# A squared-ReLU MLP in Strassen–Winograd products: one more running sum copied out of PSUM by ScalarE, the blocks of x made later, six weight tiles tagged singly

## The chip, the cores and the metric

The kernel runs on one core of a Trainium2 chip. The metric is the device time of one execution in microseconds (us). Three runs of the kernel before gave 1105.33, 1103.91 and 1101.88 us, a median of 1103.91. The core has a matrix engine (TensorE, PE in the rows), a vector engine (VectorE, DVE), a scalar engine (ScalarE, ACT), GpSimd (POOL) and SyncE (SP). The first four run instruction streams of their own and wait for each other on semaphores; in this kernel SP does nothing but issue transfers, and POOL also issues transfers that add what they bring to a tile. Matrix products land in PSUM, which the kernel uses as eight banks; everything else stands in SBUF.

## The reference

The model has two layers, d_model 1024, 512 positions, one sequence, float32. Layer 0 mixes by stick-breaking attention, layer 1 by a gated linear recurrence (RG-LRU). Each is followed by the MLP that this change is about:

```
x = x + y                                    # y: the mixer's output
h = rms_norm(x, norm_mlp[layer])             # x * rsqrt(mean(x*x) + 1e-6) * g
u = relu(h @ w1)                             # 512x1024 @ 1024x4096
x = x + (u * u) @ w2                         # 512x4096 @ 4096x1024
...
return rms_norm(x, norm_final)               # after the second layer
```

## The kernel before, in words

**Precision.** A float32 matrix is split into a high part (a cast to the type fp32r) and a low part (the matrix less its high part). A product is then three matmuls: high by high, high by low, low by high. So every operand costs a cast on ScalarE and a subtraction on VectorE; for weights these are `wh` (L971) and `wl` (L972) in `operand`, for the hidden activations `split` (L822: L825 on ScalarE, L826 on VectorE).

**The MLP (class `Mlp`, L729).** The 4096 hidden features are worked through in four quarters (`NQ`). A quarter has a first product (x by w1, then relu and square) and a second product (the squares by w2, added to the result tiles `c`).

- The first quarter's first product is dense: `squared(c)` (L790), eight chunks of 128 features, 24 matmuls of 512 columns each. Between the chunks the loop in `quarters` also puts the sums of squares for the norm (`self.sq.chunk`) and, from chunk 4 on, the *blocks of x*: `sums_of_x` (L853) scales x by the norm's gain on ScalarE and forms four block sums on VectorE, `halves_of_sums` (L876) splits these into high and low parts, and `replace` (L891), after the first second product, puts one of them where `xgh` was.
- The first products of quarters 1 to 3 are done by `up` (L896) as seven Strassen–Winograd products P1 P5 P6 P3 P7 P2 P4 of 24 matmuls each, in two halves p = 0 and 1. P1, P6, P7 and P4 add up in one PSUM bank, the running sum X; P5 and P3 in another, V; P2 stands alone, W. An intermediate value of a running sum is needed by its own: after P1, P5 and P6 ScalarE copies the bank to a tile `kept` (L922). After P3 and P7 VectorE subtracts bank and kept tile (L931, L933), after P2 it adds them (L933), and ScalarE takes relu (L934) and square (L788). P4 adds to X after P7, so it can't begin before VectorE has read X for P7.
- Each half then ends in a finishing chain: a split of three of the blocks (128 x 1536), four sums of blocks (`sums`, L828, on VectorE at L835) and two more splits of 128 x 1024. The hidden tile `u` has one buffer, which the two halves share.
- The second product is `down` (L1026): fourteen products (seven for each half g of the hidden quarter) of 12 matmuls of 512 columns. The orders stand in `ORDERS`. P5 of half 1 needs the last splits. With g = 1 the PSUM sums are scaled and added to `c` (`collect`, L1009: VectorE L1015, ScalarE L1018).

**Weights.** A product's weight is a block of w1 or w2 or a running sum of blocks. `load` (L943) issues three blocks of 512 KB on SP for each half; b21 comes through `raw` tiles in `block`. A sum of blocks is made in place by VectorE (L991), or, for P7 and P4 (the *far* products), by a transfer from POOL that accumulates (L986). The tiles have tags b11, b12 and b22 with two buffers each.

**Order.** The order of matmuls is the program's. On the other engines a list scheduler (the Tile framework) places each instruction by its own estimate of when operands are ready and by priority, which follows program order unless a `high_priority` block raises it; `issue_after` holds an instruction behind another one. Engines then run their queues strictly in order, so the instruction at the head of a queue holds up all behind it.

The last quarter of each layer goes through the `prepare` path of `down`, which prepares each weight three products ahead, and ends with `end`: in layer 0 the transposition into x for the next mixer, in layer 1 the final norm.

Of the kernel before, what the change touches and what calls it, by code (L numbers as in the profile page):

```python
# [48 lines left out]
def hybrid_encoder(  # L49
# [679 lines left out]
    class Mlp:  # L729
# [28 lines left out]
        def __init__(self, ctx, layer):  # L758
# [9 lines left out]
            self.u, self.lows, self.s3 = {}, {}, []  # L768
# [18 lines left out]
        def square(self, t):  # L787
            A.activation(t, t, AF.Square)  # L788
# [33 lines left out]
        def split(self, p, i, of, to):  # L822
            h, l = (t[:, i, to, :] for t in self.places(p))
            u = self.u[p][:, i, of, :]
            A.copy(h, u)  # L825
# [27 lines left out]
        def sums_of_x(self, k):  # L853
# [3 lines left out]
            for c in (k, C // 2 + k):  # L857
                g = col(f"mlp{self.layer}")[:, c : c + 1]
                A.activation(x[c], x[c], AF.Identity, scale=g)
            V.tensor_tensor(v[:, hi], u[:, hi], v[:, hi], ALU.subtract)  # L860
# [35 lines left out]
        def up(self, q4, p, unit, far):  # L896
# [3 lines left out]
            for name in ("P1", "P5", "P6", "P3", "P7", "P2", "P4"):  # L900
# [19 lines left out]
                if name in ("P1", "P5", "P6"):  # L920
                    t = work.tile([P, S], F32, tag="sq" if name == "P1" else "r", name="kept")
                    A.copy(t, ps)  # L922
                    kept[name] = t.rearrange("p (i n) -> p i n", i=2)
                    continue
                slot, one, op = {
                    "P3": (1, "P6", ALU.subtract), "P7": (2, "P5", ALU.subtract),
                    "P2": (0, "P1", ALU.add), "P4": (3, None, None),
                }[name]
                t = u[:, :, slot, :]
                if name == "P3":  # L930
                    V.tensor_tensor(t, three, kept[one], op)  # L931
                elif one:
                    V.tensor_tensor(t, kept[one], three, op)  # L933
                A.activation(t, t if one else three, AF.Relu)  # L934
                self.square(t)
                if name == "P2":
                    self.split(p, slice(0, 2), slice(0, 3), slice(0, 3))
            self.sums(p, slice(0, 2))
            for i in range(2):
                self.split(p, i, slice(0, 4), slice(3, 7))  # L940


        def load(self, src, far=()):  # L943

            unit = {"src": src}
            for tag in ("b11", "b12", "b22"):
                t = self.bp.tile([P, 2, S], F32, tag=tag, name=tag)
                nc.sync.dma_start(out=t.rearrange("p j n -> p (j n)"), in_=src(tag))
                unit[tag] = t
            return unit  # L950

        def from_up(self, q4, p):
            return self.load(
# [72 lines left out]
        def down(self, q4, units, far, end=None):  # L1026
# [19 lines left out]
            if end is None:  # L1046
                for at in order:
                    product(*at)
# [453 lines left out]
```

## Time and profile before

The profiled execution took 1100.71 us, of which its span, first to last instruction, is 1099.0 us; the median of the runs, 1103.91 us, is 3.2 us above it.

| view | value |
|---|---|
| TensorE busy | 1053.4 us, 96% of the span, mean granted clock 0.983 |
| VectorE busy | 867.1 us, 79% |
| ScalarE busy | 676.4 us, 62% |
| GpSimd busy | 205.1 us, 19% |
| layer 0, `down` of the first quarter and after (293 to 337 us) | TensorE 41.14 of 44.00 us, VectorE 34.98, ScalarE 21.97, clock 0.96 |
| layer 0, `up` of quarter 1 (337 to 381 us) | TensorE 41.30 of 44.00, VectorE 34.55, ScalarE 32.30, clock 1.00 |
| layer 0, `down` of quarter 1 (381 to 420 us) | TensorE 37.84 of 39.00, VectorE 32.49, ScalarE 15.50, clock 1.00 |
| layer 1, `down` of the first quarter (790 to 839 us) | TensorE 42.41 of 49.00, VectorE 37.36, ScalarE 18.55, clock 0.90 |
| layer 1, `up` of quarter 1 (839 to 882 us) | TensorE 40.32 of 43.00, VectorE 34.47, ScalarE 30.12, clock 0.97 |

A row of a timeline reads: start in us, length in us, engine, source line, operation, output tile and input tiles, shape, how many instructions in a row (x2), and in brackets the idle time of that engine before it and what ended that idle time. A row of the chain (the chain of work that ended last) gives start, length and what worked. L1004 are the matmuls of `down`, L913 those of `up`.

### The profile page before, as it was taken

Reading aid. Unit: us, or ns where it says so; the run is one execution under the profiler, and the core shown is the slowest. Engines: PE = TensorE matmul, PEld = TensorE weight load, DVE = VectorE, ACT = ScalarE, POOL = GpSimd, SP = SyncE. Lnnn points to the kernel's source line nnn. Section 1 sums busy time; section 2 is a strip of 40 time slices with the busy share of each in tenths; the row PEclk is TensorE's granted clock in tenths of the full one; section 3 lists DMA queues with packets and bytes.
Section 4 is the critical chain, followed back from the end, with each engine's and each line's share of the span. In section 5 each row is a group of like instructions: output and inputs, shape, how many; then the busy total and the mean of one; then the engine's idle time right before and its main releaser. Section 6 shows DMA issues by size and latency. Waiting matters only on the chain.

```text
span 1099.0 us, 15815 instructions
## 1 busy us (share of the span) xinstructions
PE 1053.4 (96%) x5868; PEld 912.1 (83%) x5868; DVE 867.1 (79%) x1120; ACT 676.4 (62%) x1025; POOL 205.1 (19%) x240
## 2 busy tenths in 40 slices
PE   9999999999989999999999999999979999999987
PEld 7888888888879879889877777888858888988975
DVE  7888787749876987987898778964966886887887
ACT  6767676748645745745745487855834754753655
POOL 2444443400000000000002563000000000000004
PEclk9999999999999999999999999999989999989999
DMA  7745454427366565565742784252255665655604
GB/s 237 196 119 161 116 141 114 159 87 279 89 161 152 129 181 144 134 180 146 209 77 77 176 207 134 63 187 77 58 123 164 147 140 157 156 126 153 178 3 113
DMA packets 53405, 155.22 MB, mean 141 GB/s; under 512 B 8784, under 2 KB 9552, under 8 KB 53328
## 3 DMA queue, kind: packets, MB, share of 16 engines
q1 hardware_dynamic: 43536, 120.13, 34.2%
q0 software_dynamic: 9216, 33.56, 18.7%
q8 instruction: 46, 0.75, 0.3%
q10 hardware_dynamic: 576, 0.52, 0.2%
q14 instruction: 31, 0.25, 0.1%
HBM read 132.17 MB, written 4.19 MB: 124 GB/s over the span
## 4 chain that ended last, share of the span: by engine, by line
PE 73%; DVE 13%; ACT 6%; issue 4%; DMA 2%; POOL 1%; SPq 0%; ACTq 0%; DVEq 0%; POOLq 0%
PE ps_t L913 7%; PE ps_z L913 7%; PE ps_acc L1004 6%; PE ps_t L1004 6%; PE ps_o L1004 5%; PE ps_z L1004 4%; PE ps_acc L212 4%; PE ps_acc L210 4%; PE ps_acc L211 4%; PE ps_o L913 3%; DVE wl L972 2%; ACT wh L971 2%; PE ps_o L210 2%; DVE b L991 2%; PE ps_o L212 2%
## 5 line engine op out<-in xcount | busy, mean ns | idle before, releaser
L971 ACT CAST wh<-b 128x1024 fp32r<-128x1024 f32 x168 | 174.3, 1049 | 186.6 <-DVE b L991 74.3
L972 DVE TENSOR_TENSOR wl<-b,wh 128x1024 fp32r<-128x1024 f32 x168 | 204.3, 1223 | 75.6 <-ACT wh L971 74.4
L986 POOL DMA_DIRECT2D b<-in_w_dn x30 | 26.3, 878 | 383.9 <-DVE wl L972 109.6
L198 ACT CAST wh<-raw 128x512 fp32r<-128x512 f32 (+2 forms) x88 | 69.5, 819 | 37.2 <-DMA raw<-in_w_in 10.4
L210 PE MATMUL ps_acc<-xgh,wh 128*128 128x512 f32 x208 | 85.0, 409 | 0.2 <-ACT wh L179 0.2
L205 DVE TENSOR_TENSOR wl<-raw,wh 128x512 fp32r<-128x512 f32 (+2 forms) x78 | 71.1, 938 | 16.5 <-ACT wh L198 16.3
L211 PE MATMUL ps_acc<-xgh,wl 128*128 128x512 f32 x208 | 81.5, 392 | 0.3 <-DVE wl L180 0.3
L212 PE MATMUL ps_acc<-xgl,wh 128*128 128x512 f32 x208 | 81.6, 392 | 0.1
L562 DVE TENSOR_TENSOR_SCAN scan<-keep,later 128x128 f32<-128x128 f32 (+1 forms) x64 | 58.5, 915 | 18.2 <-ACT keep L552 9.6
L986 POOL DMA_DIRECT2D b<-in_w_up x24 | 20.9, 871 | 277.3 <-DVE b L991 210.1
L991 DVE TENSOR_TENSOR b<-b,b 128x1024 f32<-128x1024 f32 x58 | 70.3, 1220 | 0.3
L566 POOL TENSOR_TENSOR w<-w,scan 128x128 f32<-128x128 f32 (+1 forms) x64 | 52.1, 815 | 55.4 <-DVE scan L562 52.5
L913 PE MATMUL ps_t<-xgh,wh 128*128 128x256 f32 x144 | 43.1, 299 | 10.8 <-ACT u L934 10.8
L972 DVE TENSOR_TENSOR wl<-raw,wh 128x1024 fp32r<-128x1024 f32 x28 | 34.2, 1223 | 18.9 <-ACT wh L971 18.8
L913 PE MATMUL ps_z<-xgh,wh 128*128 128x256 f32 x144 | 42.5, 295 | 5.4 <-DVE u L933 2.7
L835 DVE TENSOR_TENSOR u<-u 128x512 f32<-128x512 f32 (+1 forms) x80 | 46.5, 582 | 1.3
L212 PEld LDWEIGHTS ps_acc<-xgl,wh 128*128 128x128 f32 x208 | 39.0, 188 | 8.9 <-DVE xgl L119 0.5
L913 PE MATMUL ps_t<-low,wh 128*128 128x256 f32 x160 | 44.8, 280 | 0.0
L210 PEld LDWEIGHTS ps_acc<-xgh,wh 128*128 128x128 f32 x208 | 39.2, 189 | 6.6 <-ACT wh L179 0.5
L211 PEld LDWEIGHTS ps_acc<-xgh,wl 128*128 128x128 f32 x208 | 39.3, 189 | 6.3 <-DVE wl L180 0.9
L826 DVE TENSOR_TENSOR sl<-u,sh 128x1024 fp32r<-128x1024 f32 (+2 forms) x26 | 33.4, 1304 | 12.1 <-ACT sh L825 12.1
L551 ACT ACTIVATE w<-ps_z,rp 128x128 f32<-128x128 f32 (+3 forms) x56 | 29.7, 531 | 21.1 <-PE ps_z L544 18.4
(426 smaller groups left out, 3560.8 us busy)
## 6 DMA issues: line engine op xcount, KB each, us to landing
b<-in_w_dn SPq DMA_DIRECT2D x48, 512.0 KB, 5.7
b<-in_w_up SPq DMA_DIRECT2D x36, 512.0 KB, 4.0
b<-in_w_dn POOLq DMA_DIRECT2D x30, 512.0 KB, 5.5
b<-in_w_up POOLq DMA_DIRECT2D x24, 512.0 KB, 5.5
raw<-in_w_m SPq DMA_DIRECT2D x16, 512.0 KB, 3.6
raw<-in_w_dn SPq DMA_DIRECT2D x16, 512.0 KB, 4.3
raw<-in_w_in SPq DMA_DIRECT2D x16, 512.0 KB, 5.1
raw<-in_w_qk SPq DMA_DIRECT2D x12, 512.0 KB, 3.8
```

What stands on the lines that cost most here:

```text
L198: A.copy(wh[:, k, :], raw[:, k, :])
L205: V.tensor_tensor(wl[:, k, :], raw[:, k, :], f(wh[:, k, :]), ALU.subtract)
L210: PE.matmul(ps, wh, ah, start=start, stop=False)
L211: PE.matmul(ps, wl, ah, start=False, stop=False)
L212: PE.matmul(ps, wh, al, start=False, stop=stop)
L562: V.tensor_tensor_scan(sc[:, S - n : S][:, ::-1], keep[:, :n][:, ::-1], later[:, S - n :][:, ::-1], 1.0, ALU.mult, ALU.max,)
L566: G.tensor_tensor(wt, wt, sc[:, S - n + 1 : S + 1], ALU.mult)
L913: PE.matmul(ps[:, i * HS : (i + 1) * HS], m, y, start=new and i == k == n == 0, stop=i == 1 and k == C // 2 - 1 and n == 2, skip_group_che ...
L971: A.copy(wh, raw)
L972: self.cut = V.tensor_tensor(wl, raw, f(wh), ALU.subtract)
L991: self.sum = V.tensor_tensor(raw, raw, unit[to], ALU.add)
L1004: PE.matmul(ps, m, y[:, jj, cols], start=first and n == 0, stop=last and n == 2, skip_group_check=not new,)
```

## The change

1. In `up`, P7's running sum X is copied out by ScalarE like those of P1, P5 and P6 (into a `kept` tile of tag "sq"); VectorE then subtracts two SBUF tiles instead of a tile and a bank.
2. In `up`, the relu and square of P4 stand in a `high_priority` block, and so do the four sums and the last two splits.
3. `sums_of_x` and `halves_of_sums` move from the loop over `squared` into the `down` of the first quarter (after its steps 2 to 5), and `replace` goes after its step 7. `issue_after` puts the scalings behind the last high split and the first subtraction behind the last low split. `sq.chunk` is held behind the square before it.
4. The weight tiles b11, b12, b22 of the two halves have six tags b0 to b5 with one buffer each; `FROM_DOWN` and `FROM_UP` say which tile follows which. Loads are issued singly: four of the next quarter's at step 10 of `down` and two after it; of `down`'s six, three after the first half of `up` and three after the second.
5. The turn of the PSUM banks begins anew in every quarter; layer 0's last `down` uses the order "mid" instead of "last"; `prepare` holds a block sum behind the last weight difference but one (`cuts[-2]`); in layer 1's last quarter P7's block sums, too, are made by POOL's accumulating transfer.

```diff
@@ -765,7 +765,7 @@
             self.turns = count()
             self.blocks = ExitStack()
             self.bp = self.blocks.enter_context(tc.tile_pool(name=f"blocks{layer}", bufs=2))
-            self.u, self.lows, self.s3 = {}, {}, []
+            self.u, self.lows, self.s3, self.slots = {}, {}, [], None
 
             self.s41 = self.bp.tile([P, C // 2, S], F32R, tag="s41", name="s41", bufs=1)
 
@@ -785,7 +785,7 @@
             return self.u[p]
 
         def square(self, t):
-            A.activation(t, t, AF.Square)
+            self.squares = A.activation(t, t, AF.Square)
 
         def squared(self, c):
 
@@ -822,7 +822,7 @@
         def split(self, p, i, of, to):
             h, l = (t[:, i, to, :] for t in self.places(p))
             u = self.u[p][:, i, of, :]
-            A.copy(h, u)
+            self.high = A.copy(h, u)
             self.ready = V.tensor_tensor(l, u, f(h), ALU.subtract)
 
         def sums(self, p, i):
@@ -856,8 +856,10 @@
             u, v = x[k], x[C // 2 + k]
             for c in (k, C // 2 + k):
                 g = col(f"mlp{self.layer}")[:, c : c + 1]
-                A.activation(x[c], x[c], AF.Identity, scale=g)
-            V.tensor_tensor(v[:, hi], u[:, hi], v[:, hi], ALU.subtract)
+                with tc.issue_after(self.high.ins):
+                    A.activation(x[c], x[c], AF.Identity, scale=g)
+            with tc.issue_after(self.ready.ins):
+                V.tensor_tensor(v[:, hi], u[:, hi], v[:, hi], ALU.subtract)
             V.tensor_tensor(u[:, hi], u[:, lo], u[:, hi], ALU.subtract)
             V.tensor_tensor(u[:, lo], v[:, hi], u[:, lo], ALU.subtract)
             V.tensor_tensor(v[:, lo], u[:, lo], v[:, lo], ALU.add)
@@ -917,50 +919,79 @@
                                 skip_group_check=not new,
                             )
                 three = ps.rearrange("p (i n) -> p i n", i=2)
-                if name in ("P1", "P5", "P6"):
-                    t = work.tile([P, S], F32, tag="sq" if name == "P1" else "r", name="kept")
+                if name in ("P1", "P5", "P6", "P7"):
+
+                    tag = "sq" if name in ("P1", "P7") else "r"
+                    t = work.tile([P, S], F32, tag=tag, name="kept")
                     A.copy(t, ps)
                     kept[name] = t.rearrange("p (i n) -> p i n", i=2)
+                if name in ("P1", "P5", "P6"):
                     continue
-                slot, one, op = {
-                    "P3": (1, "P6", ALU.subtract), "P7": (2, "P5", ALU.subtract),
-                    "P2": (0, "P1", ALU.add), "P4": (3, None, None),
+                slot, x, y, op = {
+                    "P3": (1, three, kept.get("P6"), ALU.subtract),
+                    "P7": (2, kept.get("P5"), kept.get("P7"), ALU.subtract),
+                    "P2": (0, kept.get("P1"), three, ALU.add),
+                    "P4": (3, three, None, None),
                 }[name]
                 t = u[:, :, slot, :]
-                if name == "P3":
-                    V.tensor_tensor(t, three, kept[one], op)
-                elif one:
-                    V.tensor_tensor(t, kept[one], three, op)
-                A.activation(t, t if one else three, AF.Relu)
-                self.square(t)
-                if name == "P2":
-                    self.split(p, slice(0, 2), slice(0, 3), slice(0, 3))
-            self.sums(p, slice(0, 2))
-            for i in range(2):
-                self.split(p, i, slice(0, 4), slice(3, 7))
-
-
-        def load(self, src, far=()):
-
-            unit = {"src": src}
-            for tag in ("b11", "b12", "b22"):
-                t = self.bp.tile([P, 2, S], F32, tag=tag, name=tag)
-                nc.sync.dma_start(out=t.rearrange("p j n -> p (j n)"), in_=src(tag))
-                unit[tag] = t
-            return unit
-
-        def from_up(self, q4, p):
-            return self.load(
-                lambda tag: w_up[self.layer, q4 - 1, p, *self.SOURCES[tag]].rearrange(
-                    "p k n -> p (k n)"
-                )
+                with tc.high_priority() if name == "P4" else nullcontext():
+                    if op:
+                        V.tensor_tensor(t, x, y, op)
+                    A.activation(t, t if op else three, AF.Relu)
+                    self.square(t)
+                    if name == "P2":
+                        self.split(p, slice(0, 2), slice(0, 3), slice(0, 3))
+            with tc.high_priority():
+                self.sums(p, slice(0, 2))
+                for i in range(2):
+                    self.split(p, i, slice(0, 4), slice(3, 7))
+
+
+
+
+        FROM_DOWN = {
+            (0, "b11"): (0, "b22"), (0, "b12"): (1, "b22"), (0, "b22"): (0, "b12"),
+            (1, "b11"): (1, "b12"), (1, "b12"): (0, "b11"), (1, "b22"): (1, "b11"),
+        }
+        FROM_UP = {
+            (0, "b11"): (0, "b11"), (0, "b12"): (0, "b12"), (1, "b11"): (0, "b22"),
+            (1, "b12"): (1, "b22"), (0, "b22"): (1, "b12"), (1, "b22"): (1, "b11"),
+        }
+
+        def units(self, sources, come_from):
+
+            if self.slots is None:
+                self.slots = {at: i for i, at in enumerate(come_from)}
+            else:
+                self.slots = {at: self.slots[old] for at, old in come_from.items()}
+            return [{"src": src} for src in sources]
+
+        def load(self, units, *ats):
+            for g, tag in ats:
+                t = self.bp.tile([P, 2, S], F32, tag=f"b{self.slots[g, tag]}", name=tag, bufs=1)
+                nc.sync.dma_start(out=t.rearrange("p j n -> p (j n)"), in_=units[g]["src"](tag))
+                units[g][tag] = t
+
+        def from_up(self, q4):
+            return self.units(
+                [
+                    lambda tag, p=p: w_up[self.layer, q4 - 1, p, *self.SOURCES[tag]].rearrange(
+                        "p k n -> p (k n)"
+                    )
+                    for p in range(2)
+                ],
+                self.FROM_DOWN,
             )
 
-        def from_down(self, q4, g):
-            return self.load(
-                lambda tag: w_dn[self.layer, q4, g, *self.SOURCES[tag]].rearrange(
-                    "p j n -> p (j n)"
-                )
+        def from_down(self, q4):
+            return self.units(
+                [
+                    lambda tag, g=g: w_dn[self.layer, q4, g, *self.SOURCES[tag]].rearrange(
+                        "p j n -> p (j n)"
+                    )
+                    for g in range(2)
+                ],
+                self.FROM_UP,
             )
 
         def operand(self, raw):
@@ -1023,9 +1054,9 @@
             "last": "P1 0 P5 0 P2 0 P1 1 P2 1 P5 1 P6 0 P6 1 P3 0 P3 1 P7 0 P7 1 P4 0 P4 1",
         }
 
-        def down(self, q4, units, far, end=None):
-            sums, last_cut = {}, {}
-            order = self.ORDERS["last" if end else "mid" if q4 else "first"].split()
+        def down(self, q4, units, far, end=None, then={}):
+            sums, last_cut, ws, cuts = {}, {}, {}, []
+            order = self.ORDERS["last" if end and self.layer else "mid" if q4 else "first"].split()
             order = [(name, int(g)) for name, g in zip(order[::2], order[1::2])]
 
             def product(name, g, w=None):
@@ -1038,25 +1069,24 @@
                     self.times(name, g, i, w, sums[to][i], new)
                 if g:
 
-                    first = {"P2": self.sum, "P5": last_cut.get("P6")}.get(name) if end else None
+                    first = {"P2": self.sum, "P5": last_cut.get("P6")}.get(name) if ws else None
                     with tc.issue_after(first.ins) if first else nullcontext():
                         for i in range(2):
                             self.collect(name, i, sums[to][i])
 
             if end is None:
-                for at in order:
+                for n, at in enumerate(order):
                     product(*at)
+                    for x in then.get(n, ()):
+                        x()
                 return
-            ws = {}
-
             def prepare(name, g):
 
-                if (name, g) != ("P7", 1):
-                    self.before = self.cut
-                ahead = None
-                if (name, g) != ("P5", 0):
-                    ahead = self.ready if name == "P5" else self.before
+                ahead = cuts[-2] if len(cuts) > 1 else None
+                if (name, g) == ("P5", 1):
+                    ahead = self.ready
                 ws[name, g] = self.block(units[g], name, far, ahead)
+                cuts.append(self.cut)
                 last_cut[name] = self.cut
 
             for at in order[:3]:
@@ -1078,34 +1108,46 @@
                     self.sums(p, i)
                     self.split(p, i, slice(0, 4), slice(3, 7))
                 if c == 0:
-                    units = [self.from_down(0, g) for g in range(2)]
+                    units = self.from_down(0)
+                    self.load(units, *self.FROM_UP)
                 if c in range(1, 5):
 
-                    for n in range(2):
-                        self.sq.chunk(2 * (c - 1) + n, x[2 * (c - 1) + n], e=V)
+                    for n in range(2 * c - 2, 2 * c):
+                        with tc.issue_after(self.squares.ins):
+                            self.sq.chunk(n, x[n], e=V)
                 if c == C - 2:
                     self.rr = self.sq.inv_squares(self.bank())
                 between(c)
-                if c > 3:
-                    self.sums_of_x(c - 4)
-                if c > 4:
-                    self.halves_of_sums(c - 5)
-            self.halves_of_sums(3)
             for q4 in range(NQ):
+
+                self.turns = count(4 if q4 else 2)
                 if q4:
                     del self.u[0], self.u[1], self.a[1]
-                    for p in range(2):
-                        self.up(q4, p, units[p], self.FAR_UP)
-                        units[p] = self.from_down(q4, p)
-                last = q4 == NQ - 1
-                if last:
+                    ups = units
+                    self.up(q4, 0, ups[0], self.FAR_UP)
+                    units = self.from_down(q4)
+                    self.load(units, (0, "b11"), (0, "b12"), (1, "b11"))
+                    self.up(q4, 1, ups[1], self.FAR_UP)
+                    self.load(units, (1, "b12"), (0, "b22"), (1, "b22"))
+                if q4 == NQ - 1:
                     end.ready()
                     self.down(q4, units, far, end)
                     break
-                self.down(q4, units, self.FAR_DOWN)
+                ups = []
+
+                def first(q4=q4, ups=ups):
+                    ups += self.from_up(q4 + 1)
+                    self.load(ups, (0, "b11"), (0, "b12"), (0, "b22"), (1, "b11"))
+
+                then = {10: [first]}
                 if q4 == 0:
-                    self.replace()
-                units = [self.from_up(q4 + 1, p) for p in range(2)]
+
+                    for k in range(C // 2):
+                        then[k + 2] = [lambda k=k: self.sums_of_x(k), lambda k=k: self.halves_of_sums(k)]
+                    then[7] = [self.replace]
+                self.down(q4, units, self.FAR_DOWN, then=then)
+                units = ups
+                self.load(units, (1, "b12"), (1, "b22"))
             self.blocks.close()
 
     with ExitStack() as mctx:
@@ -1429,7 +1471,7 @@
             finish(3, 0, 2, HS)
 
         end.ready = factors
-        mlp.quarters(between, ("P4",), end)
+        mlp.quarters(between, ("P7", "P4"), end)
 
 
 
```

## The prediction

> **What bounds the kernel now.** I read the busy line first.
>
> ```profile
> span 1099.0 us, 15815 instructions
> PE 1053.4 (96%) x5868; PEld 912.1 (83%) x5868; DVE 867.1 (79%) x1120; ACT 676.4 (62%) x1025; POOL 205.1 (19%) x240
> ...
> b<-in_w_up SPq DMA_DIRECT2D x36, 512.0 KB, 4.0
> ```
>
> TensorE is the bound; a change gains only where TensorE waits. So the waits next (total us, times, longest):
>
> ```profile
> PE ps_t L913 <- ACT u L934: 10.8, 4, 2.7
> PE ps_t L1004 <- ACT sh L825: 8.2, 2, 5.8
> ```
>
> The first is part of a group of six, visible in TensorE's timeline: P4, the last product of each second half of `up`, stands 2.7 us until its running sum is read.
>
> ```profile
> 376.12 0.36 PE L913 MATMUL ps_t<-xgh,wh 128*128 128x256 f32 x1 [2.70 <-ACT u L934]
> 458.75 0.36 PE L913 MATMUL ps_z<-xgh,wh 128*128 128x256 f32 x1 [2.70 <-DVE u L933]
> 541.46 0.35 PE L913 MATMUL ps_t<-xgh,wh 128*128 128x256 f32 x1 [2.70 <-ACT u L934]
> 878.82 0.36 PE L913 MATMUL ps_t<-xgh,wh 128*128 128x256 f32 x1 [2.68 <-ACT u L934]
> 962.40 0.55 PE L913 MATMUL ps_z<-xgh,wh 128*128 128x256 f32 x1 [2.69 <-ACT u L934]
> 1046.98 0.52 PE L913 MATMUL ps_t<-xgh,wh 128*128 128x256 f32 x1 [2.68 <-ACT u L934]
> ```
>
> The other two (8.2 us) are P5 1 in the first quarters' `down`, waiting for the last split. Windows (us, busy time of PE, PEld, DVE, ACT, POOL, granted clock, DMA share, GB/s) show a second cost:
>
> ```profile
> 456.51:459.92 3.41, 1.17 (x10) 1.21 (x11) 3.41 (x5) 2.38 (x4) 0.00 (x0) 1.00 0.86 139
> 459.92:463.33 3.41, 3.41 (x18) 3.41 (x17) 2.85 (x4) 3.21 (x6) 0.08 (x1) 0.50 0.10 22
> ```
>
> A window that TensorE stood through for two thirds is followed by one at clock 0.50, which loses 3.41/2 = 1.7 us.
>
> Last, the chain: where `down` stands after P5 1 and near its end.
>
> ```profile
> 293.54 1.36 PE ps_o L1004 x6
> 311.23 2.32 PE ps_o L1004 x6
> 393.26 1.39 PE ps_o L1004 x6
> 424.88 2.83 PE ps_t L913 x24
> 476.18 1.39 PE ps_acc L1004 x6
> 481.67 2.73 PE ps_t L1004 x12
> 581.08 3.02 PE ps_acc L1004 x12
> 790.29 1.36 PE ps_o L1004 x6
> 813.38 2.13 PE ps_o L1004 x6
> 896.34 1.40 PE ps_o L1004 x6
> 980.93 1.39 PE ps_acc L1004 x6
> 1086.39 3.01 PE ps_acc L1004 x12
> ```
>
> Call T the end of P2 (P4's start less its idle): 376.12 − 2.70 = 373.42, then 456.05, 538.76, 876.14, 959.71, 1044.30. One `down` product is 2.73 (481.67), one `up` product of 24 matmuls 2.83 (424.88), 2.84 with the step to the next. Without waits P5 1 would end at T + 2.70 + 2.84 + 5 × 2.73 = T + 19.2. It ends at 393.26 + 1.39 = T + 21.23, at 476.18 + 1.39 = T + 21.52, and at T + 21.60 and T + 22.61 in layer 1. So TensorE waits some 2 us again, for the finishing chain (relu, square, first split, sums, last splits). That chain, not the stall alone, sets P5 1.
>
> **The change, part by part.** Copy of P7 and the stall. The finishing rows after T = 373.42, ScalarE then VectorE:
>
> ```profile
> 365.05 0.59 ACT L922 COPY kept<-ps_t 128x512 f32<-128x512 f32 x1 [1.29 <-PE ps_t L913]
> 375.47 1.17 ACT L934 ACTIVATE u<-u 128x512 f32<-128x512 f32 x2 [0.92 <-DVE u L931]
> 377.59 1.14 ACT L788 ACTIVATE u<-u 128x512 f32<-128x512 f32 x2
> 378.76 1.49 ACT L825 CAST sh<-u 128x1536 fp32r<-128x1536 f32 x1
> 380.63 1.05 ACT L971 CAST wh<-raw 128x1024 fp32r<-128x1024 f32 x1
> 388.01 2.00 ACT L825 CAST sh<-u 128x1024 fp32r<-128x1024 f32 x2 [2.23 <-DVE u L835]
> ...
> 374.69 0.68 DVE L931 TENSOR_TENSOR u<-ps_t,kept 128x512 f32<-128x512 f32 x1
> 380.28 1.76 DVE L826 TENSOR_TENSOR sl<-u,sh 128x1536 fp32r<-128x1536 f32 x1 [0.30 <-ACT sh L825]
> 383.09 1.41 DVE L835 TENSOR_TENSOR u<-u 128x512 f32<-128x512 f32 x2
> 386.15 1.22 DVE L991 TENSOR_TENSOR b<-b,b 128x1024 f32<-128x1024 f32 x1
> 389.02 0.75 DVE L1015 SCALAR_TENSOR_TENSOR c<-ps_acc,rr,c 128x512 f32<-128x512 f32 x1
> 390.34 2.36 DVE L826 TENSOR_TENSOR sl<-u,sh 128x1024 fp32r<-128x1024 f32 x2
> ```
>
> Twelve more copies of 0.59 on ScalarE; 62% busy, it takes them in idle time (the copy at 365.05 followed 1.29 idle). Uncovered they would cost 12 × 0.59 = 7; I take 0. The copy of P7 queues behind the two last splits of half 0 and then frees the bank some 2.5 us before P4 needs it, so P4 runs at T and ends at T + 2.84: 2.7 gained, six times, for the moment.
>
> Rows of one engine overlap a little, so steps are taken start to start: a cast 0.95 (380.63), a relu or square 0.53, a block sum or a cast's difference 1.14 (386.15), a sum 0.65, a collection 0.66.
>
> What is late next: ScalarE's queue, in the changed kernel's order of instructions, is relu of P3, relu of P4 (waits for P4's end, and all behind it with it), a weight cast, relu of P7, two squares, relu of P2, two squares, first split. Before, P4's relu stood behind that split . From T + 2.84: 0.53 + 0.95 + 0.53 + 1.06 + 0.53 + 1.06 + 1.49 gives the split's end at T + 9.0; before, 380.25 = T + 6.83. Its low part on VectorE (1.76, of which 1.68 bites) is done at T + 10.7. TensorE wants P1 1, third in `down`, at T + 2.84 + 2 × 2.73 = T + 8.3 instead of T + 11: it waits 0.7 there and, two matmuls later, some 1.3 for the low part, and is through P2 0 at T + 15.8.
>
> VectorE's order from T + 10.7 to the last sum: cast, sum, cast, block sum, sum, two collections, sum, cast, sum, i.e. 3 × 1.14 + 4 × 0.65 + 1.14 + 2 × 0.66 = 8.5, T + 19.2; a fourth cast to T + 20.3. Before, one cast fewer stood between the two splits and the start was at 380.28 = T + 6.86, not T + 9.0. Splits: ScalarE T + 20.1 and 21.1, VectorE T + 21.4 and 22.5 (before 392.70 = T + 19.3). P5 1 then waits 4.3 for the high part, 0.8 and 0.4 for the two low parts and ends at T + 24.3. Differences to before: 3.07, 2.78, 2.70, 1.69; sum +10.2.
>
> Clock: before, each P4 stall sat in a low window; after, the wait of 5.5 does so as well. [...] I take one window more per mid quarter, 4 × 1.7 = +6.8; ends 0 (as many as before) and 13.6 (two more each).
>
> Last quarters. Here the block sum of P5 1 stands behind the last splits on VectorE. Layer 0: first split T + 9.0, sums and collections (which need P1 1's end, T + 13.1) to T + 15.0, splits to T + 17.6, block sum T + 18.8, high cast T + 19.7, low T + 20.9: P5 1, wanted at T + 15.8, waits 3.9 + 0.95. Start of P4 0: T + 2.84 + 12 × 2.73 = 35.6, + 2.2 + 4.85 + 1.7 clock = T + 44.35; before 581.08 = T + 42.32: +2.0. Layer 1, whose order puts P2 1 ahead: 35.6 + 0.3 + 5.4 + 1.7 = T + 43.05 against 1086.39 = T + 42.09: +0.95.
>
> First quarters. `down` before runs 293.54 to 311.23 = 17.69 for five products (13.65): 4.0 lost, and the next row takes 2.32 for 1.37, 0.95 of clock; in layer 1 790.29 to 813.38 = 23.09, 9.4 lost and 0.76. The work on x leaves this path.
>
> ```profile
> 262.87 0.73 ACT L859 ACTIVATE x<-x,colt 128x512 f32<-128x512 f32 x1
> ```
>
> Eight such scalings, 16 short sums and 12 pairs of cast and difference now fall among `down`'s casts. After: the first collection of P1 1 and a cast stand ahead of the last split on ScalarE, so P5 1 still waits 0.55 + 0.9 in layer 0, 1.4 + 1.65 in layer 1 (plus 1.1 clock, a window lost with chance two thirds). The x work on VectorE makes four casts late (P3 0, P3 1, P7 0, P7 1) by 2.4 in sum in layer 0; in layer 1 the casts have the room. Layer 0: 3.85 − 4.95 = −1.1; layer 1: 4.15 − 10.2 = −6.05. If the x work hides fully it is 2.4 better, if it is wholly unhidden about 2.4 worse.
>
> Weights: the single tags move loads on SP ahead of or between products; a load lands 4.0 us after issue and every block I followed is issued two products (5.5) or more ahead, so 0; with that cover gone each late block costs at most its 4.0. The blocks added by POOL keep their place behind the same casts, except P7 in layer 1's last quarter, which spares VectorE one block sum: inside waits, 0 (−1.1 at most). Bank turns change no order: 0.
>
> Sum: 10.2 + 6.8 + 2.0 + 0.95 − 1.1 − 6.05 = +12.8, on the profiled 1100.71 us (span 1099.0): 1113.5. The median of runs, 1103.91, is 3.2 above that profile (its highest run 4.6), and I place the forecast between: 1115.
>
> [...] Here 2.70 us idle was enough for a window at 0.50. [...]
>
> **The rivals.** Faster: the finishing chain keeps its distance from the first subtraction (374.69 to 392.70), that is P4's relu does not hold the split up. Then the last split is at T + 19.3 rather than 22.5, 3.2 less at the four P5 1 with their windows, and P5 1 ends before T + 21. For: the same instructions with the same durations; P4's product ends at T + 2.84, not long after the first relu could start (375.47 = T + 2.05). Against: the relu, a cast and a square stand ahead of the split in the queue. Price: mids −3.7, last quarters −5.3, firsts −7.15: −16, 1084.6 on the profile's time. It decides where the split before P5 1 ends by about T + 19.5.
>
> No more half-clock windows than before: the new waits lie in pieces with matmuls between. 12.8 − 6.8 − 1.7 − 1.7 − 1.1 = +1.5: 1102.2.
>
> Two such windows for each wait: +10.2, 1124.
>
> The change does not do what it says: P7's copy comes late on ScalarE, whose queue holds the two last splits ahead of it, and P4 still stands 2.7 six times: +16, 1130. Margin 2.5 us against it.
>
> **How the numbers follow.** Forecast 0.60 (own range 1105 to 1124), faster 0.18, same 0.10, two windows 0.08, late copy 0.04. About 0.3% (3.3 us) is what a measurement can tell from no change. Range 1094 to 1129: below it about half of the faster rival, above it the late copy. Faster 0.18, same 0.10, slower 0.72.
>
> **What would show it.** Right: no 2.7 wait at P4; waits of some 4 us at P5 1 on the last splits in four `down`; first split ending near T + 9; low clock windows there; layer 1's first P5 1 waiting 3 instead of 9. Wrong: P5 1 ends before T + 21, or P4 still waits, or P3 and P7 casts in the first `down` come late by more than 5.

## The result, and the profile after

The changed kernel takes 1119.26 us (median of four runs, 1119.16 to 1119.45), the kernel before beside it 1102.89 us. The ratio is 1.0147, with a 95% interval from 1.0125 to 1.0169: 1.5% slower. The forecast was 1115 us, in a range of 1094 to 1129. The spans of the two profiled executions are 1099.0 and 1117.5 us, 18.5 us apart.

The page of the changed kernel, its span and busy line:

```profile
span 1117.5 us, 15833 instructions
PE 1059.0 (95%) x5868; PEld 910.4 (81%) x5868; DVE 865.9 (77%) x1118; ACT 680.5 (61%) x1037; POOL 201.1 (18%) x242
```

VectorE has 1.2 us less to do than before and ScalarE 4.1 us more, in a span 18.5 us longer; TensorE stands longer. Its waits (total us, times, longest):

```profile
PE ps_acc L1035 <- ACT sh L825: 18.2, 6, 4.1
PE ps_acc L1035 <- ACT wh L1002: 8.3, 2, 4.4
PE ps_t L1035 <- DVE sl L826: 5.7, 6, 1.1
PE ps_t L1035 <- ACT sh L825: 4.0, 5, 0.8
```

The six waits of 2.7 us at P4 (L913 in the kernel before) are gone, as the copy was to do. In their place stand waits of `down` (L1035): P5 1 for the last splits (18.2, the first quarters included), P5 1 of the last quarters for its weight's cast (8.3), and P1 1 for the two parts of the first split (4.0 and 5.7). The chain of the changed kernel through the second half of `up` and the first five products of `down`, quarter 1 of layer 0:

```profile
374.02 2.90 PE ps_z L915 x24
...
381.64 1.48 ACT sh L825
383.12 0.02 issue
383.15 1.76 DVE sl L826
384.90 0.17 DVE wl L1003
385.07 0.88 issue
385.96 0.68 DVE u L835
386.64 1.14 DVE wl L1003
387.78 1.14 DVE b L1022
388.91 0.60 DVE u L835
389.51 1.32 DVE c L1046 x2
390.83 0.60 DVE u L835
391.43 1.14 DVE wl L1003
392.57 0.61 DVE u L835
393.18 0.02 issue
393.20 1.05 ACT sh L825
394.26 0.04 issue
394.30 1.22 PE ps_acc L1035 x2
395.52 0.04 issue
395.56 4.63 PE ps_acc L1035 x10
400.20 4.87 PE ps_t L1035 x21
```

P4 runs at once (T = 374.02). In the rows left out its relu, a cast, two relus and four squares follow one another on ScalarE; the first split ends at 383.12 = T + 9.1 (forecast T + 9.0). Between the splits VectorE never rests: three weight differences (`wl`; the prediction calls them casts on VectorE), a block sum and two collections stand with the four sums, and the last sum is done at 393.18 = T + 19.2 (forecast T + 19.2). P5 1 begins at 394.30 = T + 20.3 and is through at 400.20 = T + 26.2, the last ten of its matmuls in 4.63 us where 2.3 is usual. They wait for the low parts, and the windows (columns as in the prediction) show the clock:

```profile
389.90:393.30 3.40, 0.37 (x2) 0.00 (x0) 3.40 (x6) 1.29 (x3) 0.32 (x1) 1.00 0.80 140
393.40:396.80 3.40, 2.46 (x5) 1.44 (x6) 3.24 (x3) 1.80 (x2) 0.46 (x1) 0.50 0.67 92
```

TensorE stood through the first while VectorE worked without a pause, and the next ran at half clock.

### The profile page after: what moved, and what is told of

Read it like the earlier page. It is cut to its first block, busy times and chain, and to the rows that moved or that the text cites. A ratio compares the mean times of both kernels' runs of the same rounds, so it can differ in the third digit from the quotient of the medians.

```text
span 1117.5 us, 15833 instructions
## 1 busy us (share of the span) xinstructions
PE 1059.0 (95%) x5868; PEld 910.4 (81%) x5868; DVE 865.9 (77%) x1118; ACT 680.5 (61%) x1037; POOL 201.1 (18%) x242
## 3 DMA queue, kind: packets, MB, share of 16 engines
q0 software_dynamic: 9504, 34.61, 19.2%
## 4 chain that ended last, share of the span: by engine, by line
PE 63%; DVE 15%; ACT 10%; issue 7%; DMA 4%; POOL 1%; SPq 0%; ACTq 0%; POOLq 0%; DVEq 0%
PE ps_t L1035 8%; PE ps_acc L1035 6%; PE ps_z L915 6%; PE ps_acc L212 4%; PE ps_acc L210 4%; PE ps_acc L211 4%; PE ps_o L915 4%; DVE wl L1003 3%; PE ps_acc L915 3%; DMA b<-in_w_up 3%; ACT wh L1002 2%; DVE c L1046 2%; DVE sl L826 2%; PE ps_o L210 2%; PE ps_o L211 2%
## 5 line engine op out<-in xcount | busy, mean ns | idle before, releaser
L198 ACT CAST wh<-raw 128x512 fp32r<-128x512 f32 (+2 forms) x88 | 69.4, 818 | 47.1 <-DMA raw<-in_w_in 10.2
L1035 PE MATMUL ps_acc<-wh,sh 128*128 128x512 f32 x64 | 31.8, 496 | 26.5 <-ACT sh L825 18.2
L1035 PE MATMUL ps_t<-wh,sl 128*128 128x512 f32 x126 | 50.1, 397 | 5.7 <-DVE sl L826 5.7
L915 PE MATMUL ps_z<-xgh,wh 128*128 128x256 f32 x192 | 54.2, 282 | 0.0
L915 PE MATMUL ps_z<-xgh,wl 128*128 128x256 f32 x192 | 54.2, 282 | 0.0
L1035 PE MATMUL ps_t<-wh,sh 128*128 128x512 f32 x126 | 50.1, 398 | 4.0 <-ACT sh L825 4.0
L915 PE MATMUL ps_acc<-low,wh 128*128 128x256 f32 x192 | 53.7, 280 | 0.0
L1035 PE MATMUL ps_t<-wl,sh 128*128 128x512 f32 x126 | 49.8, 395 | 0.2 <-DVE wl L1003 0.2
L1035 PE MATMUL ps_t<-wh,bh 128*128 128x512 f32 x126 | 49.6, 394 | 0.0
L1035 PE MATMUL ps_t<-wl,bh 128*128 128x512 f32 x126 | 49.2, 391 | 0.0
L1035 PE MATMUL ps_t<-wh,bl 128*128 128x512 f32 x126 | 49.2, 390 | 0.0
```

Source lines behind the costliest of these rows:

```text
L198: A.copy(wh[:, k, :], raw[:, k, :])
L915: PE.matmul(ps[:, i * HS : (i + 1) * HS], m, y, start=new and i == k == n == 0, stop=i == 1 and k == C // 2 - 1 and n == 2, skip_group_che ...
L1035: PE.matmul(ps, m, y[:, jj, cols], start=first and n == 0, stop=last and n == 2, skip_group_check=not new,)
```

## The experiments

**Which part of the change costs.** Three runs take it apart. First the copy alone, put into the kernel before:

```diff
-                if name in ("P1", "P5", "P6"):
+                if name in ("P1", "P5", "P6", "P7"):
...
-                    V.tensor_tensor(t, kept[one], three, op)
+                    V.tensor_tensor(t, kept[one], kept["P7"] if name == "P7" else three, op)
```

> The kernel before with one edit: P7's sum is copied out by ScalarE and VectorE subtracts two SBUF tiles. Theory (the copy frees the bank, but P4's relu and the cast that waits for P4's end then stand ahead of the first split on ScalarE and a cast more stands in VectorE's chain): no 2.7 us wait at P4, but P5 1 of the four middle quarters ends 1.7 to 3 us later and leaves one or two half-clock windows, last quarters +1 to +2 each, first quarters as before. Sum of what the changed kernel lost in those places: +18 and +4, so about 1124 us (1117 to 1128). Rival (the copy is a gain and the loss comes from the loads, the tags or the x blocks): -16 by the stalls taken away, about 1087, at most 1103.

Measured: 1122.79 us (1122.33 to 1123.44), 1.0195 of the kernel before (1.0167 to 1.0222). The copy alone makes the whole loss. The chain of its quarter 1 is that of the changed kernel, and no other edit is needed for it: P5 1 begins at T + 20.3 here too.

```profile
374.63 2.90 PE ps_t L913 x24
...
394.90 1.22 PE ps_z L1005 x2
```

Then the changed kernel without the copy, all else as changed:

```diff
-                if name in ("P1", "P5", "P6", "P7"):
+                if name in ("P1", "P5", "P6"):
...
-                    "P7": (2, kept.get("P5"), kept.get("P7"), ALU.subtract),
+                    "P7": (2, kept.get("P5"), three, ALU.subtract),
```

> The changed kernel with the copy of P7 undone (VectorE subtracts from the bank again); x blocks, tags, loads and bank turns as changed. Theory: six 2.7 us waits at P4 are back, the waits at P5 1 of the middle quarters shrink to the 2 us of before, the first quarters keep their gain (0.4 and 5.4 in the changed kernel's trace): about 1103 - 6 = 1097 us (1093 to 1101). Rival (loads and tags cost): 1105 or more.

Measured: 1103.25 us (1099.26 to 1107.77), 1.0020 (0.9999 to 1.0041): no gain. And the x blocks alone, in the kernel before (`sums_of_x`, `halves_of_sums` and `replace` moved as in the change):

> The kernel before with one edit: the blocks of x are made in the first quarter's down, as in the changed kernel. Theory: only the two first quarters differ; P5 1's waits of 2.7 + 0.5 and 6.2 + 1.0 us shrink to 1 to 2 us each, minus casts made late in layer 0: about 6 us less than before, 1097 us (1094 to 1100), the same as the run without the copy. Rival (x work in down makes casts late as much as it frees the splits): 1103.

Measured: 1106.17 us (1099.72 to 1109.60), 1.0047 (1.0025 to 1.0069): slower. Both expectations missed. The waits at P5 1 did shrink (counted from the start of layer 1's first `down`, P5 1 ends 4.5 us earlier in both traces), but `up` gave it back: in the run without the copy `up` of quarter 1 lasts 47.9 us in layer 0 and 49.3 us in layer 1, in the changed kernel 41.7 and 40.4, in the kernel before 42.4 and 44.3. The executions traced took 1107.77 and 1109.39 us, near the top of their ten, so they show more of this loss than most. Of the run with the x blocks alone, a row of ScalarE in quarter 1's `up`, and the wait that follows on TensorE:

```profile
351.27 2.00 ACT L973 CAST wh<-b 128x1024 fp32r<-128x1024 f32 x2 [3.80 <-DMA b<-in_w_up]
...
357.31 0.36 PE L915 MATMUL ps_z<-xgh,wh 128*128 128x256 f32 x1 [1.94 <-DVE u L935]
```

A block that comes late holds ScalarE, VectorE waits for the cast, its subtraction for P7 comes late behind it, and without the copy P4 waits for that subtraction. So the copy does something that I had not counted: it takes VectorE's lateness off TensorE's path in `up`. In these traces that is why the x blocks pay in the changed kernel and not alone. Such a block is one that POOL adds; here POOL issues it at 344.17, where the kernel before does at 340.13, so it lands late mostly because it is issued late; what held the work ahead of it was not followed to its end. These two kernels spread over 8 and 10 us from run to run, as the kernel before does (7.6 us in the 19 runs beside them), the changed one over 0.3; why some executions are later than others was not settled. The tags, the loads and the bank turns were not run alone.

**What makes the finishing chain late.** The prediction blamed ScalarE's queue (P4's relu ahead of the first split) and VectorE's longer list between the splits, without telling the shares apart. One run holds the relu, and the cast that waits for P4's end, behind the split (`early` is the first split):

```diff
-                    A.activation(t, t if op else three, AF.Relu)
+                    with tc.issue_after(self.high.ins) if name == "P4" else nullcontext():
+                        A.activation(t, t if op else three, AF.Relu)
...
+            late = {order[3]: self.early} if q4 else {}
...
+            with tc.issue_after(behind.ins) if behind else nullcontext():
+                A.copy(wh, raw)
```

> The changed kernel with two holds on ScalarE: P4's relu, and the one weight cast that waits for P4's end (the fourth product of down), stand behind the first split of the half. Theory A (ScalarE's queue is what makes the finishing chain late): the first split ends 2 us earlier, at T + 6.9 instead of T + 9.0, the waits of 1.0 and 1.2 us at P1 1 go, and P5 1 ends 2 us earlier: 6 times 2 us, about 1107 us (1104 to 1110). Theory B (VectorE, which stands without a pause from the first subtraction to the last split, sets the chain; the split's place on ScalarE only moves its idle time): the waits at P1 1 go and come back at P5 1, since five casts, a block sum and two collections now stand between the splits on VectorE: P5 1 ends near T + 24.5 as before, 1116 to 1121.

Measured: 1124.39 us (1122.84 to 1126.41), 1.0221 (1.0200 to 1.0243): theory A falls. ScalarE and TensorE of that run:

```profile
380.80 1.49 ACT L825 CAST sh<-u 128x1536 fp32r<-128x1536 f32 x1
394.65 1.99 ACT L825 CAST sh<-u 128x1024 fp32r<-128x1024 f32 x2 [2.69 <-DVE u L835]
...
395.75 0.79 PE L1038 MATMUL ps_acc<-wh,sh 128*128 128x512 f32 x1 [6.33 <-ACT sh L825]
```

The first split begins at 380.80, 0.8 us earlier than in the changed kernel although the second half of `up` ends 0.7 us later, and the last ones begin at 394.65, 1.5 us later, after 2.69 us in which ScalarE waited for VectorE's sums. What ScalarE gained, VectorE's list took: it now has five weight differences, a block sum and two collections there.

Next VectorE is cleared, with the order of the products unchanged; `ready` is the low part of the last split there, so the collections of P1 1 and P2 1 go behind it:

```diff
+                    if q4 and name in ("P1", "P2"):
+                        first = self.ready
...
+            nth = order.index(("P5", 1)) + 1
+            late = {order[3]: self.early, order[nth]: self.high} if q4 else {}
...
+            with tc.issue_after(self.ready.ins) if behind is self.high else nullcontext():
+                self.cut = V.tensor_tensor(wl, raw, f(wh), ALU.subtract)
...
+                hold = self.cut if q4 and (name, g) == order[nth + 1] else None
...
-                if (name, g) == ("P5", 1):
-                    ahead = self.ready
```

> As the run before, and besides VectorE is cleared for the chain: the two collections of P1 1 and P2 1, the weight difference of P6 0 and the block sum of P6 1 are held behind the last splits, and in the last quarters P5 1's block sum no longer waits for them. Order of the products unchanged. Theory B: between the first split's low part (T + 8.6) and the last splits VectorE has two casts and four sums, so the last splits are done at T + 16.8 instead of T + 22.5 and P5 1 ends at T + 18.4 instead of T + 24.3; with half-clock windows gone, 6 or 7 us in each of six places: 1078 us (1070 to 1090), under the kernel before. Rival (the deferred casts make P6 and P3 as late as P5 1 was): within 5 us of the changed kernel.

Measured: 1090.92 us (1089.19 to 1093.31), 0.9918 (0.9895 to 0.9940): 0.8% under the kernel before and, by the ratios, 2.3% (25 us) under the changed kernel. VectorE between the splits, and what is left at P5 1:

```profile
381.42 1.76 DVE L826 TENSOR_TENSOR sl<-u,sh 128x1536 fp32r<-128x1536 f32 x1 [0.30 <-ACT sh L825]
383.10 1.22 DVE L1007 TENSOR_TENSOR wl<-raw,wh 128x1024 fp32r<-128x1024 f32 x1
384.23 1.22 DVE L1007 TENSOR_TENSOR wl<-b,wh 128x1024 fp32r<-128x1024 f32 x1
385.37 2.86 DVE L835 TENSOR_TENSOR u<-u 128x512 f32<-128x512 f32 x4
389.34 2.36 DVE L826 TENSOR_TENSOR sl<-u,sh 128x1024 fp32r<-128x1024 f32 x2 [1.11 <-ACT sh L825]
...
389.36 0.50 PE L1039 MATMUL ps_acc<-wh,sh 128*128 128x512 f32 x1 [0.85 <-ACT sh L825]
```

P5 1's wait falls from 4.03 to 0.85 us, and in the four middle quarters' `down` no half-clock window is left. The expectation of 1078 was too low: the first split ended 0.9 us later than I walked it, and P6 0 and P6 1 wait for weight differences that were put off (3.4 and 3.6 us for products of 2.7).

The same without the two holds on ScalarE (P4's relu and the cast stand ahead of the split again; the cast of P6 0's weight is still held behind the last splits, together with its difference):

> The chain-first run without its two holds on ScalarE: P4's relu and the cast that waits for P4's end stand ahead of the first split again, as in the changed kernel; only VectorE's holds are left. Theory B (VectorE's order alone sets P5 1): the first split ends at T + 9.0 again and P1 1 waits some 2 us, but then only one cast and four sums stand ahead of the last splits, which are done near T + 17.7, and P5 1 ends near T + 19 as in the chain-first run: 1091 us (1086 to 1095). Theory A (P4's relu ahead of the split is what costs, and VectorE's holds pay only together with it): 1100 or more.

Measured: 1094.46 us (1093.12 to 1096.51), 0.9936 (0.9912 to 0.9961). Its splits on ScalarE:

```profile
380.79 1.48 ACT L825 CAST sh<-u 128x1536 fp32r<-128x1536 f32 x1
388.01 2.00 ACT L825 CAST sh<-u 128x1024 fp32r<-128x1024 f32 x2 [4.80 <-DVE u L835]
```

T is 373.00 here and 373.50 in the run before, so the first split begins 1.4 us later than there and the last ones only 0.25 us later. By the ratios VectorE's order makes 2.1 of the 2.3%, ScalarE's holds at most the rest; the intervals of the two runs overlap.

**Whether a later P5 1 helps.** The order "last" puts one more product ahead of P5 1. On the changed kernel:

```diff
-            order = self.ORDERS["last" if end and self.layer else "mid" if q4 else "first"].split()
+            order = self.ORDERS["last" if q4 else "first"].split()
```

> The changed kernel with one edit: down of quarters 2 and 3 of each layer and of layer 0's last takes the order "last", in which P2 0 and P2 1 stand ahead of P5 1, so that TensorE reaches P5 1 one product (2.7 us) later. [...] Rival (the chain hangs on TensorE's products by the collections that stand among the sums, and slides with them): within 3 us of the changed kernel, 1116 to 1120.

Measured: 1120.31 us (1119.41 to 1121.73), 1.0173 (1.0145 to 1.0201); the rival holds. The theory, that the wait of 4.3 us at P5 1 shrinks, stood at 1101 us (1097 to 1106). And with VectorE cleared:

> As the run before with the order "last" in all second products after the first quarter's. P5 1 comes one product later, but one block sum and two casts more stand in VectorE's chain (last splits at T + 19.2, P5 1 ends at T + 20.3 with one product less to go, equal to T + 17.6 in the other order): within 5 us of the run before, rather below, 1075 us (1068 to 1085). Rival (VectorE is the bound of the whole stretch, so that a later P5 1 only draws more casts in): 3 us or more above it.

Measured: 1101.05 us (1096.99 to 1108.53), 1.0006 (0.9983 to 1.0029), 10 us above the run with the order unchanged. Its first wait is now

```profile
PE ps_t L1039 <- DVE wl L1007: 7.9, 8, 1.9
...
484.85 0.50 PE L1039 MATMUL ps_t<-wl,sh 128*128 128x512 f32 x1 [1.88 <-DVE wl L1007]
```

that is mostly P6 1 for its weight's difference (6.7 of the 7.9 us; `sh` is half 1). VectorE has nearly as much to do for each product as TensorE (32.49 against 37.84 us in the `down` of quarter 1 before); a product drawn forward brings its casts and its collections along, and the time is lost at the next product.

**What the half clock costs.** Twelve matmuls without use fill P5 1's wait in the four middle quarters:

```diff
+                if (name, g) == ("P5", 1) and q4 in (1, 2):
+                    for spare in (bank("o"), bank("o")):
+                        for n in range(6):
+                            PE.matmul(
+                                spare, self.a[0][0][:, 0, 0, :P], xgh[:, 0, :],
+                                start=n == 0, stop=n == 5,
+                            )
```

> The changed kernel with 12 matmuls of 512 columns (2.7 us, into banks that down leaves free, result unused) put ahead of P5 1 in the four middle quarters, inside its wait of 4.3 us. They price the clock. Theory (a window with TensorE standing for two thirds is followed by one at half clock): no half-clock window after P5 1, 1.2 to 1.4 us less in each of four places: 1114 us (1112 to 1116). Rival (the half clock costs nothing, because what runs in it waits for the splits anyway): 1119; or the added work delays P5 1: 1121 or more.

Measured: 1115.17 us (1114.96 to 1115.66), 1.0138 (1.0117 to 1.0159); the ratios overlap, and the times, 4.1 us below the changed kernel's, come from another chip. The two traces bear the expectation out: spans 1113.3 and 1117.5, and the last matmul 4.2 us earlier. The gain stands where the matmuls were put: the four middle `down` are 5.7 us shorter together, with two half-clock windows in them (both after P1 1's waits) in place of seven. P5 1's window in quarter 1 of layer 0 is now busy and at full clock:

```profile
392.41:395.82 3.41, 3.41 (x15) 2.36 (x13) 3.41 (x4) 2.82 (x3) 0.88 (x1) 1.00 0.56 91
```

More work on TensorE, less time.

**What the copy is worth once VectorE is cleared.** The holds alone in the kernel before, and then with the copy. Of the other parts of the change both runs have one, the order "mid" in layer 0's last `down`:

> The kernel before with the holds of the chain-first run alone (no copy of P7, x blocks, tags and loads as before). Theory (VectorE's order sets P5 1; without the copy TensorE comes to P5 1 2.7 us later, so only the 2 us wait there can go, while the six waits at P4 stay and P6 0 waits about 1.5 us for its deferred cast): 0.5 to 2 us less in each of six places, about 1096 us (1092 to 1100). Rival (the holds alone make the gain of the chain-first run, and the copy adds nothing to it): 1091 or less.

Measured: 1098.17 us (1095.64 to 1101.74), 0.9976 (0.9954 to 0.9998).

> The kernel before with the copy of P7 and the holds; x blocks, tags, loads and bank turns as before. Theory (the copy pays once VectorE is cleared for the chain; the x blocks pay another 0.4 and 5.4 us in the first quarters, as in the changed kernel's trace): about 6 us above the chain-first run, 1097 us (1093 to 1100). Rival (moved x blocks and single tags are worth nothing, as in the run of the x blocks alone): 1089 to 1092, as the chain-first run.

Measured: 1095.26 us (1091.87 to 1098.66), 0.9946 (0.9927 to 0.9966). By the ratios: holds −0.2%, with the copy −0.5%, with the x blocks, tags and loads −0.8%. The copy, +2.0% by itself, gains some 0.3% with the holds; the intervals of neighbouring steps overlap, so only the whole way from the first step to the last is clear of the noise.

A last hold, the second collection of P1 1 behind P6 0's difference:

> The chain-first run with one more hold: of the two collections of P1 1, which stand ahead of P6 0's weight difference on VectorE, the second comes after it. P6 0 waited 0.7 us for that difference in the chain-first run. Theory: 0.66 us earlier in four or five places, 1088 us (1086 to 1091). Rival (the second collection is then what P6 0 waits for): same within 2 us.

Measured: 1092.19 us (1088.66 to 1096.88), 0.9923 (0.9897 to 0.9949): the same as without it, as the rival said.

## Why the prediction was right

The forecast held because the chain after the copy was walked in the changed order, engine by engine. Its terms against the traces (T is the start of P4 after, the end of P2 before):

| step | forecast | measured |
|---|---|---|
| waits of P4 in the second halves | none | none |
| P5 1's end, four middle quarters, clock included | 10.2 + 6.8 = +17.0 | 4.95 + 3.74 + 4.60 + 3.56 = +16.9 |
| P4 0's start, last quarters | +2.0 and +0.95 | +3.3 and +1.85 |
| first `down`, layer 0 | −1.1 | −2.4 |
| first `down`, layer 1 | −6.05 | −5.4 |

The measured second row comes from these rows of the changed kernel's chain, P4's start and P6 0's start, beside those already shown (quarter 2 of each layer here; quarter 1 of layer 1 has 882.82 and 909.02):

```profile
461.48 2.90 PE ps_z L915 x24
486.74 5.48 PE ps_t L1035 x24
...
971.38 2.89 PE ps_z L915 x24
997.55 5.60 PE ps_t L1035 x24
```

They give T + 25.26, T + 26.20 and T + 26.17, less the T + 21.52, 21.60 and 22.61 of before. That the second row agrees to 0.1 us is partly luck. Between T and P5 1's end the four quarters have seven half-clock windows after and four before, three more and not four; by the forecast's own price of 1.7 us for a window that leaves 11.7 us for the waits, where 10.2 were forecast. That every wait of 4.3 us brings one window more, the ground of the +6.8, is shown by no run: of the six stalls of 2.7 us at P4 before, five had half clock in them or within 1.2 us of their end and the one that ended at 376.12 had none, and in the four quarters after there are 6.83, 3.41, 6.83 and 6.83 us of it. One by one the quarters were forecast at +4.8, +4.5, +4.4 and +3.4. In layer 1's first quarter P5 1 waited in two pieces, forecast as 1.4 and 1.65:

```profile
814.94 0.50 PE L1035 MATMUL ps_acc<-wh,sh 128*128 128x512 f32 x1 [1.38 <-ACT sh L825]
817.11 0.80 PE L1035 MATMUL ps_acc<-wh,sl 128*128 128x512 f32 x1 [1.43 <-DVE sl L826]
```

The sum fell 5.7 us short (12.8 against 18.5 between the spans). Beside the differences of the table, places priced at nothing moved. Layer 0's first `down` gained 2.4 us, more than forecast, but the `up` after it lost 2.0 again: the price of 0 for the loads and for the blocks added by POOL, which "keep their place behind the same casts", failed there. The casts themselves came later. The second of these blocks was issued at 341.26 and took 6.69 us to land, not the 4.0 of SP's loads; before it was issued at 340.13, though `up` began 1.65 us later. ScalarE waited for it 0.79 us before (first row) and 3.47 us after:

```profile
346.70 1.05 ACT L971 CAST wh<-b 128x1024 fp32r<-128x1024 f32 x1 [0.79 <-DMA b<-in_w_up]
...
341.26 6.69 DMA b<-in_w_up
...
348.03 2.00 ACT L1002 CAST wh<-b 128x1024 fp32r<-128x1024 f32 x2 [3.47 <-DMA b<-in_w_up]
```

And 1.3 us went to one half-clock window in the recurrence, which the change does not touch (below). The rest, in pieces of at most 1.2 us at the start, in later `up` and after the last matmul, was not followed.

One step was wrong, though the sum did not show it: the price of the faster rival, "P4's relu does not hold the split up". The relu does stand ahead of the split, but moving it back gained nothing; what counts is the list of VectorE between the splits. The same walk held the answer: T + 9.1 to T + 19.2 is VectorE's time, and P4's relu is not in it. The forecast also never asked what the copy does for `up` when VectorE is late, which the two runs without it showed.

## What to carry to other kernels

When a stall is taken away, walk the changed instruction order from that place to the next one where the bound engine waits: here TensorE came 2.7 us earlier to data that a scheduler had just made 2 to 3 us later, and a copy that did exactly what it said made the kernel slower. Among engines that feed a chain, look for the one that never idles in it, and reorder that one; work moved off ScalarE's queue here only moved its idle time (2.69 us before the last splits). A reordering and a removal of a stall can each be worth little or less than nothing and yet pay together, so they are to be tried together.

## What the runs showed of the hardware

In these runs the length of a wait alone did not decide whether half clock came with it; what does was not shown (the six stalls of 2.7 us above, and the rows below). In the clock that the profiles record, the half-clock stretches inside the kernel before last 3.41, 6.83 or 10.24 us, those inside the changed kernel 3.41 or 6.83. In the recurrence TensorE has a wait of 2.22 us before and of 2.21 us after; the first row of each pair has the end of that wait in it, the second is the stretch behind:

```profile
664.70:668.10 3.40, 1.96 (x7) 1.34 (x8) 2.66 (x5) 2.21 (x3) 0.31 (x1) 1.00 0.88 231
668.10:671.50 3.40, 3.40 (x16) 2.77 (x16) 2.46 (x4) 3.38 (x6) 0.00 (x0) 1.00 0.86 196
```

```profile
673.30:676.70 3.40, 1.19 (x6) 0.69 (x5) 2.66 (x5) 0.94 (x2) 1.60 (x2) 1.00 0.39 99
676.70:680.10 3.40, 3.40 (x9) 2.40 (x9) 2.91 (x5) 2.82 (x5) 0.00 (x0) 0.50 0.98 224
```

The first pair is the kernel before (busy 1.96 of 3.40, clock 1.00 after), the second the changed one (1.19 of 3.40, clock 0.50). From the first matmul behind the wait to the tenth it is 2.48 us before (666.14 to 668.62) and 3.79 us after (676.43 to 680.22). So an edit elsewhere moved 1.3 us into code that it does not touch. In layer 1's first quarter two gaps of 1.38 and 1.43 us, with two matmuls between them, came with clock 0.50 from 816.62 to 820.03: the matmul at 817.11 takes 0.80 us where the one at 814.94 took 0.50.
